# Where operand tiles lie in SBUF: a two-layer attention and FFN trunk on one core

## The chip, the cores and the metric

The kernel runs on one core of a Trainium2 chip. The metric is device time in microseconds. Three runs of the kernel before took 1240.68 to 1240.99 us, median 1240.82.

## What is computed

The input x is 512 tokens by 1024, float32. Two layers follow, each with a mixing half and an FFN half, and a last RMS norm:

```python
for l in range(DEPTH):                                   # 2
    h = rms_norm(x, norm1_g[l])
    rq, rk, rv, rg, sq, sk, sv = split(h @ w_in[l])      # 1024 x 3584
    ret = chunk_retention(rotary(rq), rotary(rk), rv)    # 4 heads of 128
    ret = head_group_norm(ret, ret_norm_g[l]) * silu(rg)
    sb  = head_rms_norm(stick_breaking(sq, sk, sv), sb_norm_g[l])   # 4 heads of 128
    x = x + concat([ret, sb]) @ w_out[l]                 # 1024 x 1024
    h = rms_norm(x, norm2_g[l])
    x = x + (silu(h @ w_gate[l]) * (h @ w_up[l])) @ w_down[l]       # 1024 <-> 2816
return rms_norm(x, final_g)
```

## The kernel before

**Split operands.** Every float32 operand of a large product is kept as two tiles of type fp32r, `hi` and `lo`, made by a ScalarE cast and a VectorE (or GpSimd) subtraction (`split`, L270 to L281). A block of a product is then three matmuls, hi x hi, hi x lo and lo x hi (`mm3`, L181), of 128 x 128 stationary by 128 x 512 moving columns in the projections.

**Stages.** x lies transposed in eight tiles of 128 x 512 (`x0` to `x7`), and so do its gained copies `hhi` and `hlo`. The weights come in 205 units of 1024 columns, in the order of their use (`block_plan`): DMA to `wraw`, split to `whi` and `wlo` three units ahead (`WeightStream`, L94 to L140). In a layer the order is: SV by token; SQ, SK and RG by head; RV by token; RQ and RK by head; the output projection, its first half over the four stick-breaking heads, its second over the four retention heads; then gate and up for 11 of the 22 blocks of the FFN (`f`), down for these, and the same again for the other 11. In the first layer down has the weights stationary and the gated activations (`ahi`, `alo`) moving (L704); in the second the activations are stationary and 512 weight columns moving (`step`, L717).

**Order.** TensorE's program order is written out by hand (`Stream`): the projections are the main stream, and scores, transposes and weighted sums of the heads are side tasks put in after a delay. A scheduler orders the other engines. Each head's scores and weights become pairs (`pthi`, `ptlo`, L438), its result `m` is normed by `shi`, `slo` and a sum over ones (`normed`, L457), and split to `mhi`, `mlo`, which the output projection reads.

**Pools.** A tile pool is a stretch of every partition; pools lie one above the other in the order of their opening. `const`, `keep`, `wpool` and `small` stay; the pools `at0`, `ff0`, `at1` and `ff1` are opened above them one at a time and share the same room. As the built program has it, in KiB from the start of a partition (a 128 x 512 tile takes 2 KiB):

| what | before | after |
|---|---|---|
| scratch that the program reserves for dynamic DMA | 0 to 16 | 0 to 1 |
| constants (`ident`, `ones_r`, ...) | 16 to 19.3 | 1 to 4.3 |
| x | 19.3 to 35.3 | 112.3 to 128.3 |
| `hhi`, `hlo` | 35.3 to 67.3 | 4.3 to 36.3 |
| `ssq`, `rs` | 67.3 to 71.3 | 128.3 to 132.3 |
| `wraw` | 71.3 to 83.3 | 132.3 to 144.3 |
| `whi`, `wlo` | 83.3 to 107.3 | 36.3 to 60.3 |
| temporaries of `small` | 107.3 to 115.7 | 144.3 to 152.7 |
| attention: `vhi`, `vlo` | 127.8 to 143.8 | 60.3 to 76.3 (slots 0 to 7) |
| attention: `qhi`, `qlo`, `khi`, `klo` | 145.8 to 155.8 | 76.3 to 84.3 (slots 8 to 11) |
| attention: `pthi`, `ptlo` | 161.8 to 173.8 | 84.3 to 96.3 (slots 12 to 17) |
| attention: `mhi`, `mlo` of retention heads | 185.8 to 217.8 | 96.3 to 112.3 (slots 18 to 25) |
| attention: `mhi`, `mlo` of stick-breaking heads | 185.8 to 217.8 | 186.8 to 202.8 |
| attention: `shi`, `slo` | 181.8 to 185.8 | 182.8 to 186.8 |
| FFN: `ahi`, `alo`, first layer | 123.8 to 167.8 | 60.3 to 104.3 (slots 0 to 21) |
| FFN: `ahi`, `alo`, second layer | 143.9 to 187.9 | 60.3 to 104.3 (slots 0 to 21) |

Of the kernel before, what the change touches and what calls it, by code (L numbers as in the profile page):

```python
# [10 lines left out]
F32 = mybir.dt.float32  # L11
# [24 lines left out]

# the triangle of score blocks, by bank: block rows of [query, key], and of [key, query]
BY_QUERY = ((3,), (2, 0), (1,))
# [4 lines left out]


def block_plan():
    """Weight blocks in the order of their use: (tensor, layer, k tile, column, width)."""
    plan = []
# [46 lines left out]
class WeightStream:  # L94
    """Loads the weights ahead of their use and splits each into two 12-bit parts."""

    AHEAD = 3

    def __init__(self, nc, pool, ws):
        self.nc, self.pool, self.ws = nc, pool, ws  # L100
        self.units = unit_plan()
        self.raw = []
        self.ready = []
        self.at = (0, 0, 0)

    def load(self, upto, step=UW):
        for i in range(len(self.raw), min(upto, len(self.units))):
            w = sum(b[4] for b in self.units[i])
            raw = self.pool.tile([P, UW], F32, tag="wraw", name=f"wraw{i}", bufs=3)
            for a in range(0, w, step):  # L110
                c = slice(a, min(a + step, w))
                self.nc.sync.dma_start(out=raw[:, c], in_=self.ws[i, :, c])
            self.raw.append((raw, w))
# [28 lines left out]
class Stream:  # L142
    """The order of the tensor engine's work: side tasks are put into the main stream
    when enough of it has passed for their operands to be ready."""

# [53 lines left out]
def layers(ctx, tc, xT_in, ws_in, gcol_in, gfin_in, cos_in, sin_in, dec_in, out):  # L199
    nc = tc.nc  # L200
    const = ctx.enter_context(tc.tile_pool(name="const", bufs=1))
    keep = ctx.enter_context(tc.tile_pool(name="keep", bufs=1))
    wpool = ctx.enter_context(tc.tile_pool(name="wpool", bufs=3))
    small = ctx.enter_context(tc.tile_pool(name="small", bufs=3))
    pp = ctx.enter_context(tc.tile_pool(name="psum", bufs=1, space=PSUM))

    pe = Stream(nc)
    wst = WeightStream(nc, wpool, ws_in)
    NG = 24

    def table(inst):
        """Keeps the scalar engine's table functions in the order of the program."""
        tc.stamp_issue_order_token(inst.ins, "table")
        return inst
# [40 lines left out]

    hhi = [keep.tile([P, S], F32R, name=f"hhi{k}", tag=f"hhi{k}") for k in range(KT)]
    hlo = [keep.tile([P, S], F32R, name=f"hlo{k}", tag=f"hlo{k}") for k in range(KT)]
    ssq = keep.tile([P, S], F32, name="ssq")
# [23 lines left out]
    def feed(k, g):  # L282
        """x tile k is complete: its gained and split copy, and its squares."""
        split(hhi[k], hlo[k], x[k], gcol[:, g + k : g + k + 1])
        if k == 0:
            nc.scalar.activation(out=ssq, in_=x[k], func=AF.Square)
        else:
            q = small.tile([P, S], F32, tag="sqx", name="sqx", bufs=2)
            nc.scalar.activation(out=q, in_=x[k], func=AF.Square)  # L289
            nc.gpsimd.tensor_tensor(out=ssq, in0=ssq, in1=q, op=ALU.add)  # L290

    def rsqrt(out, ss, n, act=nc.scalar.activation):
        """out = (ss / n + eps) ** -0.5, from exp and ln and a Newton step."""
        shape = list(ss.shape)
# [15 lines left out]
    def token_scale():  # L310
        """rs[:, t] = rsqrt(mean of x[t]^2 + eps), the same on every partition."""
        hi, lo = (small.tile([P, S], F32R, tag="sqx", name=n, bufs=2) for n in ("sshi", "sslo"))
        split(hi, lo, ssq)
        ps = bank("o", 1)
        pe.mm(ps, ones_r, hi, True, False)
        pe.mm(ps, ones_r, lo, False, True)
        rsqrt(rs, ps, DM, act)
# [11 lines left out]
    def attention(l):  # L329
        g0 = l * NG  # L330
        with tc.tile_pool(name=f"at{l}", bufs=1, reuse_waits="tile") as sb:
# [25 lines left out]
            def proj_v(col, evac):  # L357
                """[token, column] products, the last k tiles by token block."""
                pss = banks_a() if col == SV else [bank() for _ in range(3)] + [bank("z", 4)]
                v = [  # L360
                    sb.tile([P, TB, S], F32R, tag=n, name=n, bufs=1) for n in ("vhi", "vlo")
                ]
# [11 lines left out]
                for tb in range(TB):  # L374
                    for k, w in ws:
                        step(tb, k, w)
                    done.append(tb)
                    if col == SV and tb == 0:
                        continue
                    if col == SV and tb == 1:  # L380
                        scales()
                    while done:
                        i = done.pop(0)
                        evac(i, pss[i], v[0][:, i], v[1][:, i])
                return v
# [19 lines left out]
            def parts(t, tag):  # L405
                hi = sb.tile([P, S], F32R, tag=tag + "hi", name=tag + "hi", bufs=1)
                lo = sb.tile([P, S], F32R, tag=tag + "lo", name=tag + "lo", bufs=1)
                split(hi, lo, t, eng=nc.gpsimd)
                return t, hi, lo
# [11 lines left out]
            def outer(ps, a, b, ca, cb, last=True):  # L421
                """ps = a[:, ca].T @ b[:, cb] for split a and b."""
                n = cb.stop - cb.start
# [7 lines left out]
            def piece(name, dtype, tag, n, bufs):  # L431
                return sb.tile([P, S], dtype, tag=tag, name=name, bufs=bufs)[:, :n]

            def pair(src):
                n = src.shape[-1]
                hi, lo = (piece(t, F32R, t, n, 3) for t in ("pthi", "ptlo"))
                split(hi, lo, src)
                return hi, lo  # L438

            def weighted(wt, v, h):  # L440
                """o[e, t] = sum over s of v[s, e] wt[s, t], by blocks of s."""
                o = bank("o", 1)
                e = slice(h * HD, h * HD + HD)
                for js, (hi, lo) in zip(BY_KEY, wt):
                    a = 0
                    for j in js:
                        c = slice(a, a + S - j * P)
                        a = c.stop
                        pe.mm3(
                            o[:, j * P :], (v[0][:, j, e], v[1][:, j, e]), (hi[:, c], lo[:, c]),  # L450
                            j == 0, j == BY_KEY[-1][-1],
# [5 lines left out]
            def normed(o, m, key):  # L457
                """m, o by head with its gains, times the rsqrt of o's mean squares."""
                sq = temp("sq")
# [5 lines left out]
                def finish():  # L465
# [5 lines left out]
                    nc.vector.tensor_tensor(out=m, in0=m, in1=rn, op=ALU.mult)  # L471
                    hi = sb.tile([P, S], F32R, tag="mhi", name="mhi", bufs=8)
                    lo = sb.tile([P, S], F32R, tag="mlo", name="mlo", bufs=8)
                    split(hi, lo, m)
# [143 lines left out]
    def ffn(l):  # L618
        last = l == L - 1
        with tc.tile_pool(name=f"ff{l}", bufs=1, reuse_waits="tile") as sb:  # L620
# [39 lines left out]
            def gated(f, pg, pu):  # L660
# [5 lines left out]
                nc.vector.tensor_tensor(out=u, in0=u, in1=g, op=ALU.mult)  # L666
                hi = sb.tile([P, S], F32R, tag=f"ahi{f % FH}", name="ahi")
                lo = sb.tile([P, S], F32R, tag=f"alo{f % FH}", name="alo")
                split(hi, lo, u)
# [127 lines left out]
```

## Time and profile before

| | |
|---|---|
| median of 3 runs | 1240.82 us |
| span of the profiled execution, first to last instruction | 1238.8 us |
| TensorE (PE) busy | 1220.4 us, 99% |
| PE weight loads (PEld), beside the matmuls | 999.2 us, 81% |
| VectorE (DVE), ScalarE (ACT), GpSimd (POOL) busy | 56%, 39%, 13% |
| mean granted clock of TensorE | 0.994 |

The profile shows one execution, whose own time is its span; the median of the runs is 2.0 us above it. Matmuls are pipelined, so the "mean ns" of a matmul (some 390 ns) counts a good part of its time together with the next one's. The pace of a row of matmuls is read from start to start: the time between the starts of the first and of a later one, by the number of matmuls between them.

### The profile page before, as it was taken

To read this page: it belongs to the slowest core of one execution; us is meant where nothing else is said; L and a number is where in the kernel's file an instruction comes from. 1 tells how busy PE (TensorE), PEld (TensorE's weight loads), DVE (VectorE), ACT (ScalarE), POOL (GpSimd) and SP (SyncE) were. 2 spreads that over 40 slices of the span, in tenths; PEclk is the share of its full clock that TensorE was granted. 3 is DMA by queue.
4 is the path that set the end of the run, shared out by engine and by line. 5 is a ranking of instruction groups with operands and counts; after the bars stand their busy time and mean duration, and the time that the engine had idled before them with its cause. 6 is when DMAs were issued, how large, how long until landed. Compare 5 with 4: busy or idle time off the path is not lost.

```text
span 1238.8 us, 13898 instructions
## 1 busy us (share of the span) xinstructions
PE 1220.4 (99%) x5474; PEld 999.2 (81%) x5474; DVE 693.5 (56%) x861; ACT 488.8 (39%) x708; POOL 165.7 (13%) x142
## 2 busy tenths in 40 slices
PE   8999999999999999999999999999999999999997
PEld 5888887888888888888888888878888888888886
DVE  5557799775443244444444778997644433444433
ACT  5557553453322123223334766345432312223323
POOL 3221154130000000000112212422100000000011
PEclk9999999999999999999999999999999999999999
DMA  6221231232322323322232222223322322332221
GB/s 238 86 80 57 85 102 58 80 101 87 102 100 87 102 86 101 102 93 96 91 129 86 69 69 85 85 69 102 103 85 89 99 83 94 113 102 87 101 85 69
DMA packets 33329, 115.74 MB, mean 93 GB/s; under 512 B 3824, under 2 KB 3824, under 8 KB 33264
## 3 DMA queue, kind: packets, MB, share of 16 engines
q1 hardware_dynamic: 33120, 114.83, 28.1%
q8 instruction: 43, 0.70, 0.2%
q14 instruction: 22, 0.18, 0.0%
q10 hardware_dynamic: 144, 0.02, 0.0%
HBM read 112.75 MB, written 2.10 MB: 93 GB/s over the span
## 4 chain that ended last, share of the span: by engine, by line
PE 94%; DVE 4%; issue 1%; DMA 1%; ACT 1%; POOL 0%; SPq 0%; DVEq 0%; ACTq 0%
PE acc L178 72%; PE z L178 16%; PE o L178 5%; PE z L189 1%; DMA wraw<-ws 1%; DVE ptlo L274 1%; DVE wlo L125 1%; DVE hlo L277 0%; DVE u L300 0%; DVE mlo L274 0%; POOL slo L274 0%; DVE m L561 0%; DVE t L416 0%; DVE t L414 0%; DVE p L552 0%
## 5 line engine op out<-in xcount | busy, mean ns | idle before, releaser
L124 ACT CAST whi<-wraw 128x1024 fp32r<-128x1024 f32 (+1 forms) x205 | 214.6, 1047 | 505.7 <-PE acc L178 237.2
L178 PE MATMUL acc<-hhi,whi 128*128 128x512 f32 x960 | 376.0, 392 | 0.0
L178 PE MATMUL acc<-hhi,wlo 128*128 128x512 f32 x960 | 373.9, 389 | 0.0
L178 PE MATMUL acc<-hlo,whi 128*128 128x512 f32 x960 | 373.6, 389 | 0.0
L125 DVE TENSOR_TENSOR wlo<-wraw,whi 128x1024 fp32r<-128x1024 f32 (+1 forms) x205 | 258.1, 1259 | 135.8 <-ACT whi L124 134.7
L178 PEld LDWEIGHTS acc<-hhi,wlo 128*128 128x128 f32 x960 | 180.2, 188 | 37.8
L178 PEld LDWEIGHTS acc<-hhi,whi 128*128 128x128 f32 x960 | 180.3, 188 | 36.2
L178 PEld LDWEIGHTS acc<-hlo,whi 128*128 128x128 f32 x960 | 180.3, 188 | 36.0
L665 DVE TENSOR_TENSOR u<-acc,rs 128x512 f32<-128x512 f32 x40 | 27.7, 692 | 134.5 <-PE acc L178 134.5
L290 POOL TENSOR_TENSOR ssq<-ssq,sqx 128x512 f32<-128x512 f32 x28 | 44.8, 1600 | 397.0 <-ACT sqx L289 396.3
L662 DVE TENSOR_TENSOR g<-acc,rs 128x512 f32<-128x512 f32 x40 | 27.7, 692 | 89.9 <-PE acc L178 89.9
L178 PE MATMUL acc<-ahi,wlo 128*128 128x512 f32 x176 | 69.8, 396 | 0.0
L178 PE MATMUL acc<-alo,whi 128*128 128x512 f32 x176 | 69.8, 396 | 0.0
L178 PE MATMUL acc<-ahi,whi 128*128 128x512 f32 x176 | 69.8, 396 | 0.0
L730 POOL TENSOR_TENSOR xtd<-xtd,gfin 128x512 f32<-128x512 f32 x7 | 10.1, 1447 | 349.3 <-ACT fsq L726 349.3
L277 DVE SCALAR_TENSOR_TENSOR hlo<-x,gcol,hhi 128x512 fp32r<-128x512 f32 x32 | 38.6, 1224 | 9.0 <-ACT hhi L276 9.0
L178 PEld LDWEIGHTS acc<-alo,whi 128*128 128x128 f32 x176 | 33.1, 188 | 8.1
L178 PEld LDWEIGHTS acc<-ahi,whi 128*128 128x128 f32 x176 | 33.1, 188 | 8.1
L178 PEld LDWEIGHTS acc<-ahi,wlo 128*128 128x128 f32 x176 | 33.1, 188 | 8.1
L273 ACT CAST ahi<-u 128x512 fp32r<-128x512 f32 x44 | 27.3, 621 | 28.1 <-DVE u L666 28.1
L178 PE MATMUL acc<-mhi,wlo 128*128 128x512 f32 x88 | 36.2, 411 | 0.0
L178 PE MATMUL acc<-mlo,whi 128*128 128x512 f32 x88 | 36.0, 409 | 0.0
(189 smaller groups left out, 1819.0 us busy)
## 6 DMA issues: line engine op xcount, KB each, us to landing
wraw<-ws SPq DMA_DIRECT2D x203, 512.0 KB, 3.5
x<-xT SPq DMA_DIRECT2D x8, 256.0 KB, 7.4
dec<-dec SPq DMA_DIRECT2D x8, 256.0 KB, 4.1
out<-ob SPq DMA_DIRECT2D x4, 512.0 KB, 2.6
wraw<-ws SPq DMA_DIRECT2D x2, 256.0 KB, 3.8
cosrs<-cos SPq DMA_DIRECT2D x2, 256.0 KB, 5.3
sinrs<-sin SPq DMA_DIRECT2D x2, 256.0 KB, 5.4
gfin<-gfin SPq DMA_DIRECT2D x1, 512.0 KB, 4.5
```

Of the source, the lines that this page charges most:

```text
L124: nc.scalar.copy(out=hi[:, c], in_=raw[:, c])
L125: nc.vector.tensor_tensor(out=lo[:, c], in0=raw[:, c], in1=hi[:, c].bitcast(F32), op=ALU.subtract)
L178: self.nc.tensor.matmul(ps, lhsT=lhsT, rhs=rhs, start=start, stop=stop)
L189: self.nc.tensor.transpose(out, src, ident)
L273: nc.scalar.copy(out=hi, in_=src)
L274: eng.tensor_tensor(out=lo, in0=src, in1=hi.bitcast(F32), op=ALU.subtract)
L277: eng.scalar_tensor_tensor(out=lo, in0=src, scalar=scale, in1=hi.bitcast(F32), op0=ALU.mult, op1=ALU.subtract,)
L290: nc.gpsimd.tensor_tensor(out=ssq, in0=ssq, in1=q, op=ALU.add)
L662: nc.vector.tensor_tensor(out=g, in0=pg, in1=rs, op=ALU.mult)
L665: nc.vector.tensor_tensor(out=u, in0=pu, in1=rs, op=ALU.mult)
L730: nc.gpsimd.tensor_tensor(out=y, in0=y, in1=gfin[:, c], op=ALU.mult)
```

## The change

Three new pools stand below `keep`: `hpool` takes `hhi` and `hlo`, `wpool` keeps only `whi` and `wlo`, and `low` has 26 slots of 128 x 512. The slots take the tiles `vhi`, `vlo` (now four tiles each, one for each block of 128 tokens), `qhi` to `klo`, `pthi`, `ptlo` and the retention heads' `mhi`, `mlo` in attention, and the activations `ahi`, `alo` in the FFN. x, `ssq`, `rs`, `wraw` and all temporaries come above them. The scratch for dynamic DMA goes from 16 KiB to 1 KiB. Not moved down are the stick-breaking heads' `mhi`, `mlo`, the tiles `shi`, `slo`, and the float32 tiles that TensorE transposes or reads whole (`e`, `q`, `k`, x, `ssq`). No operation is added or removed. The diff, cut:

```diff
     const = ctx.enter_context(tc.tile_pool(name="const", bufs=1))
+    hpool = ctx.enter_context(tc.tile_pool(name="hpool", bufs=1))
+    wpool = ctx.enter_context(tc.tile_pool(name="wpool", bufs=3))
+    low = ctx.enter_context(tc.tile_pool(name="low", bufs=1))
     keep = ctx.enter_context(tc.tile_pool(name="keep", bufs=1))
-    wpool = ctx.enter_context(tc.tile_pool(name="wpool", bufs=3))
+    rawpool = ctx.enter_context(tc.tile_pool(name="rawpool", bufs=3))
...
+V_SLOT, QK_SLOT, PT_SLOT, M_SLOT = 0, 8, 12, 18
+    def slot(i, name):
+        return low.tile([P, S], F32R, tag=f"slot{i}", name=name)
...
-            raw = self.pool.tile([P, UW], F32, tag="wraw", name=f"wraw{i}", bufs=3)
+            raw = self.rawpool.tile([P, UW], F32, tag="wraw", name=f"wraw{i}", bufs=3)
...
-    hhi = [keep.tile([P, S], F32R, name=f"hhi{k}", tag=f"hhi{k}") for k in range(KT)]
+    hhi = [hpool.tile([P, S], F32R, name=f"hhi{k}", tag=f"hhi{k}") for k in range(KT)]
...
                 v = [
-                    sb.tile([P, TB, S], F32R, tag=n, name=n, bufs=1) for n in ("vhi", "vlo")
+                    [slot(V_SLOT + TB * i + tb, n) for tb in range(TB)]
+                    for i, n in enumerate(("vhi", "vlo"))
                 ]
...
-                hi, lo = (piece(t, F32R, t, n, 3) for t in ("pthi", "ptlo"))
+                at = PT_SLOT + 2 * (pairs[0] % 3)
+                pairs[0] += 1
+                hi, lo = slot(at, "pthi")[:, :n], slot(at + 1, "ptlo")[:, :n]
...
-                    hi = sb.tile([P, S], F32R, tag="mhi", name="mhi", bufs=8)
-                    lo = sb.tile([P, S], F32R, tag="mlo", name="mlo", bufs=8)
+                    if key < NH:
+                        hi, lo = (slot(M_SLOT + 2 * key + i, n) for i, n in enumerate(("mhi", "mlo")))
+                    else:
+                        hi = sb.tile([P, S], F32R, tag="mhi", name="mhi", bufs=4)
+                        lo = sb.tile([P, S], F32R, tag="mlo", name="mlo", bufs=4)
...
-                hi = sb.tile([P, S], F32R, tag=f"ahi{f % FH}", name="ahi")
-                lo = sb.tile([P, S], F32R, tag=f"alo{f % FH}", name="alo")
+                hi, lo = slot(2 * (f % FH), "ahi"), slot(2 * (f % FH) + 1, "alo")
...
-    nc = bacc.Bacc("TRN2", target_bir_lowering=False, num_devices=1)
+    nc = bacc.Bacc("TRN2", target_bir_lowering=False, num_devices=1, dynamic_dma_scratch_size=1024)
```

TensorE's instructions and GpSimd's stand in the same order as before. On the other engines the scheduler moves a few. On VectorE, at the start of the first layer's RQ and RK projections, the rows before are these (`wlo21` to `wlo23` are splits of weight units, `rn` belongs to the norm of the last stick-breaking head, `t1` and `t2` to the rotation of the first RQ head):

```order
L274 TENSOR_TENSOR vlo_1137<-vtmp_1324,vhi_1136 128x512
L399 TENSOR_TENSOR vtmp_1344<-vtmp_1344,mu_1346 128x512
L300 SCALAR_TENSOR_TENSOR u_1376<-r_1375 128x512
L303 SCALAR_TENSOR_TENSOR u_1376<-o_1371,u_1376 128x512
L274 TENSOR_TENSOR vlo_1137<-vtmp_1344,vhi_1136 128x512
L306 SCALAR_TENSOR_TENSOR rn_1374<-u_1376,r_1375 128x512
L414 TENSOR_TENSOR t1_1399<-acc_1352,cosrs_203 128x512
L125 TENSOR_TENSOR wlo23_1412<-wraw23_1357,whi23_1411 128x1024
L415 TENSOR_TENSOR t2_1400<-acc_1352,sinrs_204 64x512
```

and in the changed kernel, at the same place of the same engine, they are these:

```order
L285 TENSOR_TENSOR vlo_1157<-vtmp_1345,vhi_1153 128x512
L411 TENSOR_TENSOR vtmp_1365<-vtmp_1365,mu_1367 128x512
L311 SCALAR_TENSOR_TENSOR u_1397<-r_1396 128x512
L285 TENSOR_TENSOR vlo_1158<-vtmp_1365,vhi_1154 128x512
L314 SCALAR_TENSOR_TENSOR u_1397<-o_1392,u_1397 128x512
L128 TENSOR_TENSOR wlo23_1433<-wraw23_1378,whi23_1432 128x1024
L317 SCALAR_TENSOR_TENSOR rn_1395<-u_1397,r_1396 128x512
L426 TENSOR_TENSOR t1_1420<-acc_1373,cosrs_212 128x512
L427 TENSOR_TENSOR t2_1421<-acc_1373,sinrs_213 64x512
```

The split `wlo23` moved ahead of `rn` and `t1`, and stands ahead of `t2` in both; a few rows earlier `wlo21` moved behind one subtraction, and on ScalarE two small casts moved ahead of the cast of a weight unit. The second layer has the same moves. On the DMA queue of SyncE, towards the end of the first layer's FFN, the loads of the next layer's rotation tables (`cosrs`, `sinrs`) and of the first two decay tables (`dec`) stood here before:

```order
L112 DMA wraw105_4653<-ws 128x1024
L112 DMA wraw106_4683<-ws 128x1024
L340 DMA cosrs_4640<-cos 128x512
L341 DMA sinrs_4641<-sin 128x512
L537 DMA dec_5963<-dec 128x512
L537 DMA dec_6096<-dec 128x512
L112 DMA wraw107_4713<-ws 128x1024
```

and stand here now:

```order
L115 DMA wraw95_4307<-ws 128x1024
L115 DMA wraw96_4342<-ws 128x1024
L351 DMA cosrs_4661<-cos 128x512
L352 DMA sinrs_4662<-sin 128x512
L556 DMA dec_5996<-dec 128x512
L556 DMA dec_6129<-dec 128x512
L115 DMA wraw97_4379<-ws 128x1024
```

They moved ahead of ten weight loads; the load of `gfin` in the second layer moved ahead of two.

## Rows read from the trace of the kernel before

**Rows 1.** The page, part 1: busy us (share of the span) and instructions

```profile
span 1238.8 us, 13898 instructions
PE 1220.4 (99%) x5474; PEld 999.2 (81%) x5474; DVE 693.5 (56%) x861; ACT 488.8 (39%) x708; POOL 165.7 (13%) x142
```

**Rows 2.** The page, part 4: the chain that ended last, by engine

```profile
PE 94%; DVE 4%; issue 1%; DMA 1%; ACT 1%; POOL 0%; SPq 0%; DVEq 0%; ACTq 0%
```

**Rows 3.** Waits of TensorE: who waited for whom, us in total, times, longest

```profile
PE z L178 <- DVE wlo L125: 3.2, 3, 2.7
PE o L178 <- ACT shi L273: 2.6, 2, 1.3
PE o L178 <- POOL slo L274: 2.1, 2, 1.1
```

**Rows 4.** Timeline of TensorE (start us, busy us): where FFN stretches begin

```profile
377.01 0.40 PE L178 MATMUL acc<-ahi,whi 128*128 128x512 f32 x1
...
438.85 0.39 PE L178 MATMUL acc<-hhi,whi 128*128 128x512 f32 x1
...
558.55 0.40 PE L178 MATMUL acc<-ahi,whi 128*128 128x512 f32 x1
...
620.39 0.39 PE L178 MATMUL z<-whi,hhi 128*128 128x512 f32 x1
...
988.29 0.39 PE L178 MATMUL acc<-whi,ahi 128*128 128x512 f32 x1
...
1049.88 0.39 PE L178 MATMUL acc<-hhi,whi 128*128 128x512 f32 x1
...
1169.58 0.39 PE L178 MATMUL acc<-whi,ahi 128*128 128x512 f32 x1
...
1230.94 0.40 PE L178 MATMUL z<-whi,alo 128*128 128x512 f32 x1
```

**Rows 5.** Groups by line, 438.85 to 558.5 and 377.01 to 438.8 us: one of three

```profile
L178 PE MATMUL acc<-hhi,whi 128*128 128x512 f32 x176 | 68.5, 389 | 0.0
...
L178 PE MATMUL acc<-ahi,whi 128*128 128x512 f32 x88 | 34.9, 396 | 0.0
```

**Rows 6.** Stretches: length, busy us of PE, PEld, DVE, ACT, POOL; PEclk, DMA, GB/s

```profile
378.00:438.00 60.00, 60.00 (x258) 48.24 (x257) 19.32 (x20) 11.22 (x12) 0.00 (x0) 1.00 0.29 95
440.00:558.00 118.00, 118.00 (x522) 97.76 (x521) 53.41 (x63) 34.17 (x42) 0.00 (x0) 1.00 0.30 98
```

**Rows 7.** Timeline of TensorE: output projection of the first layer, and a side task

```profile
227.85 0.39 PE L178 MATMUL o<-pthi,vhi 128*128 128x512 f32 x1
...
228.54 0.33 PE L178 MATMUL o<-pthi,vhi 128*128 128x384 f32 x1
...
236.51 0.39 PE L178 MATMUL z<-mhi,whi 128*128 128x512 f32 x1
...
256.80 0.39 PE L178 MATMUL z<-hhi,whi 128*128 128x512 f32 x1
```

**Rows 8.** Groups of ScalarE by line: high addresses only, low addresses only

```profile
L273 ACT CAST ahi<-u 128x512 fp32r<-128x512 f32 x44 | 27.3, 621 | 28.1 <-DVE u L666 28.1
L289 ACT ACTIVATE sqx<-x 128x512 f32<-128x512 f32 x28 | 17.1, 616 | 0.0
```

**Rows 9.** The page, part 5: splits of the weights, and projections that read the hi tiles

```profile
L124 ACT CAST whi<-wraw 128x1024 fp32r<-128x1024 f32 (+1 forms) x205 | 214.6, 1047 | 505.7 <-PE acc L178 237.2
L178 PE MATMUL acc<-hhi,whi 128*128 128x512 f32 x960 | 376.0, 392 | 0.0
...
L125 DVE TENSOR_TENSOR wlo<-wraw,whi 128x1024 fp32r<-128x1024 f32 (+1 forms) x205 | 258.1, 1259 | 135.8 <-ACT whi L124 134.7
```

**Rows 10.** Waits of SyncE's DMA queue: us in total, times, longest

```profile
SPq L112 <- DVE wlo L125: 1088.4, 197, 12.3
```

**Rows 11.** A stretch of the first layer: length, PE busy; PEclk, DMA share, GB/s

```profile
204.00:207.00 3.00, 3.00 (x9) 0.55 0.00 0
```

More of the change, by code (lines that the diff above doesn't have):

```diff
@@ L97, with __init__ @@
     AHEAD = 3
-    def __init__(self, nc, pool, ws):
-        self.nc, self.pool, self.ws = nc, pool, ws
+    def __init__(self, nc, pool, rawpool, ws):
+        self.nc, self.pool, self.rawpool, self.ws = nc, pool, rawpool, ws
         self.units = unit_plan()
@@ L207, in layers @@
     pe = Stream(nc)
-    wst = WeightStream(nc, wpool, ws_in)
+    wst = WeightStream(nc, wpool, rawpool, ws_in)
+    def slot(i, name):
+        return low.tile([P, S], F32R, tag=f"slot{i}", name=name)
     NG = 24
@@ L254, in layers @@
     )
-    hhi = [keep.tile([P, S], F32R, name=f"hhi{k}", tag=f"hhi{k}") for k in range(KT)]
-    hlo = [keep.tile([P, S], F32R, name=f"hlo{k}", tag=f"hlo{k}") for k in range(KT)]
+    hhi = [hpool.tile([P, S], F32R, name=f"hhi{k}", tag=f"hhi{k}") for k in range(KT)]
+    hlo = [hpool.tile([P, S], F32R, name=f"hlo{k}", tag=f"hlo{k}") for k in range(KT)]
     ssq = keep.tile([P, S], F32, name="ssq")
@@ L383, in proj_v @@
                         i = done.pop(0)
-                        evac(i, pss[i], v[0][:, i], v[1][:, i])
+                        evac(i, pss[i], v[0][i], v[1][i])
                 return v
@@ L405, in parts @@
             def parts(t, tag):
-                hi = sb.tile([P, S], F32R, tag=tag + "hi", name=tag + "hi", bufs=1)
-                lo = sb.tile([P, S], F32R, tag=tag + "lo", name=tag + "lo", bufs=1)
+                at = QK_SLOT + 2 * "qk".index(tag)
+                hi, lo = slot(at, tag + "hi"), slot(at + 1, tag + "lo")
                 split(hi, lo, t, eng=nc.gpsimd)
@@ L432, in piece @@
                 return sb.tile([P, S], dtype, tag=tag, name=name, bufs=bufs)[:, :n]
+            pairs = [0]
             def pair(src):
                 n = src.shape[-1]
-                hi, lo = (piece(t, F32R, t, n, 3) for t in ("pthi", "ptlo"))
+                at = PT_SLOT + 2 * (pairs[0] % 3)
+                pairs[0] += 1
+                hi, lo = slot(at, "pthi")[:, :n], slot(at + 1, "ptlo")[:, :n]
                 split(hi, lo, src)
@@ L449, in weighted @@
                         pe.mm3(
-                            o[:, j * P :], (v[0][:, j, e], v[1][:, j, e]), (hi[:, c], lo[:, c]),
+                            o[:, j * P :], (v[0][j][:, e], v[1][j][:, e]), (hi[:, c], lo[:, c]),
                             j == 0, j == BY_KEY[-1][-1],
```

## The prediction

> **What bounds the kernel now.** I read the busy times first, then the chain, then TensorE's waits. TensorE is busy 1220.4 of 1238.8 us [rows 1], and the chain that ended last is 94% TensorE [rows 2]. Its three largest waits sum to 3.2 + 2.6 + 2.1 = 7.9 us in the whole span [rows 3]. So the end is set by how fast TensorE takes one matmul after the other, and a change that alters no instruction of it can only act through that pace or through waits.
>
> The pace is not in the mean durations, which overlap; it is read from start to start. Gate and up of the first layer's second half run from 438.85 to 558.55 us [rows 4] with 3 x 176 = 528 matmuls [rows 5]: 119.70 / 528 = 226.7 ns. Down of the half before runs from 377.01 to 438.85 us [rows 4] with 3 x 88 = 264 matmuls of the same shape [rows 5]: 61.84 / 264 = 234.2 ns. In the second layer down takes 1049.88 - 988.29 = 61.59 us for 264 [rows 4], 233.3 ns.
>
> What differs? Both stretches have TensorE at full clock and without a gap, and the same DMA share, 0.29 and 0.30; the faster one has the busier neighbours, VectorE at 53.41 / 118 = 45% against 19.32 / 60 = 32%, ScalarE at 29% against 19% [rows 6]. So the slower pace isn't other engines' traffic. The pattern is the same too, three matmuls per block. What is left is where the operands lie. Gate and up read `hhi`, `hlo` and the split weights, all between 35 and 107 KiB of the partition; down reads `ahi`, `alo` between 124 and 188 KiB, moving in the first layer and stationary in the second (the names in [rows 4] stand as moving, stationary). The second half of the output projection, whose moving `mhi`, `mlo` lie above 185 KiB, bears it out: from 236.51 to 256.80 us [rows 7] stand 87 matmuls of 512 columns (the 96 of the half less 9 already past), 20.29 / 87 = 233.2 ns. No row tells whether the upper part itself is slow or the distance between the two operands; the change brings both down, so it doesn't matter here. Nor does a row tell where the step lies, only that it is between 107.3 KiB (end of `wlo`) and 123.8 (first `ahi`). The slots end at 112.3; were the step right at 107.3, the last retention head's `mhi` and `mlo` would stay slow, 2 x 24 matmuls, 0.3 us.
>
> **The change, part by part.** I take 226.7 ns for a matmul both of whose operands come to lie in the lower part.
>
> Down, four stretches: at that pace 264 matmuls take 59.85 us. The first layer's two took 61.84 each (377.01 to 438.85, 558.55 to 620.39), the second's 61.59 and, for 263 intervals, 1230.94 - 1169.58 = 61.36 against 59.62 [rows 4]. Gain 1.99 + 1.99 + 1.74 + 1.74 = 7.46 us. TensorE has no gap there and nothing else waits, so it comes whole.
>
> Output projection: only the retention heads' half moves down, 96 matmuls a layer: 2 x 96 x (233.2 - 226.7) ns = 1.25 us. The stick-breaking half, as many, keeps its pace.
>
> Scores and weighted sums, 32 tasks: the three matmuls of 512 columns in one go at (228.54 - 227.85) / 3 = 230 ns [rows 7], 3.3 ns over the fast pace: 32 x 3 x 3.3 ns = 0.3 us. The narrower ones could gain too: a task of about 1.9 us by the same 2.8% that the output projection gains, 32 tasks, 1.7 us; the low end is nothing. I take 0.3, the value of its own row.
>
> What moves up: x, raw weights, temporaries. ScalarE's pass over 128 x 512 takes 621 ns with both sides high and 616 ns with both sides low [rows 8], so its work and VectorE's keep their times. If the 205 weight casts took 5 ns more each, that were 1 us of ScalarE, covered by its idle time of 505.7 us ahead of just these casts, most of it waiting for TensorE to free a buffer [rows 9]. x's 32 transposes, slowed as down is, would cost 32 x 7.5 ns = 0.2 us. I put both at nothing.
>
> The moved instructions: on VectorE a split of 1259 ns [rows 9] goes ahead of `rn` and `t1`. Behind `rn` waits the last stick-breaking head's `mhi`, read in the output projection; GpSimd's sum of `t1` and `t2` is no later, since `t2` stood behind that split before. The weight unit behind a small cast comes some 0.6 us later [rows 8]; TensorE's only wait for splits is 3.2 us in three times [rows 3], and three units are ahead. On the DMA queue four small loads pass ten weight loads; the queue waits 1088.4 us for VectorE to free raw buffers [rows 10], so it has time, and no wait in front of these four is new. `v` in four tiles makes waits finer, not later. Price of all this: nothing; if the cover were gone, one late split, 1.3 us a layer.
>
> The waits for `shi` and `slo` stay, since the chain through ScalarE and GpSimd isn't touched. After them the granted clock averages 0.55 from 204 to 207 us [rows 11], 9 matmuls in 3.00 us where 13 fit at 226.7: 4 x 0.227 = 0.9 us there. If TensorE reaches them sooner, it waits longer by that much, at most the 0.3 us of the tasks; a lost or gained wait with its slow clock is worth up to (2.6 + 2.1) / 2 + 0.9 = 3.3 us a layer.
>
> Sum: 7.46 + 1.25 + 0.3 = 9.0 us. The profiled span becomes 1238.8 - 9.0 = 1229.8; the median stands 2.0 us above the span, so 1240.8 - 9.0 = 1231.8 us.
>
> **Rivals.** *The place has no part in it.* Then the time stays at 1240.8. For it: no row shows one and the same matmul with its operand low and high, and the slow ones also share that their operand was made a short while before. Against it: in down each activation tile is read eight times, over 61.8 us, and the pace doesn't recover; and `hhi` is made anew four times without being slow. [...]
>
> *The bottom of the partition is slow as well.* `hhi` and `hlo` go from 35 to 67 KiB down to 4 to 36, from where no 512-column fp32r operand was streamed before. If they took on down's pace there, 3 x 960 = 2,880 matmuls [rows 9] would lose 6.9 ns each, 19.9 us: 1231.8 + 19.9 = 1251.7, slower. It decides from 9.0 / 0.0069 = 1,300 such matmuls on. Against it: `hhi0` to `hlo7` and the weights stream evenly over 72 KiB.
>
> *Only the moving operand counts, or waits eat a part.* Then the second layer's 3.48 us, where the activations are stationary, don't come: 1235.3. Against it: that stretch is slow now with its moving operand low.
>
> **How the numbers follow.** Forecast as summed 0.80; no effect 0.09; slow bottom 0.05; part of it 0.06. A measurement of this kernel tells a change from none at about 0.2%, 2.5 us. The forecast and the part are faster by more: 0.86. No effect gives 0.08 within 0.2% and, with its last hundredth and the slow bottom, 0.06 slower. The likeliest one's own range is 1229.0 (tasks gain 1.7 instead of 0.3, and 1.4 of the 3.3 that a wait with its clock is worth goes) to 1234.4 (a late split in each layer adds 2.6). Taking in the partial case, 1235.3 with one late split of 2.6, the range is 1229.0 to 1238.0; left out are no effect and the slow bottom, 0.14.
>
> **What would show it.** Right: starts 226 to 228 ns apart in all four down stretches (some 59.9 us for 264) and in the second half of the output projection; gate and up unchanged at 119.7 us; the stick-breaking half of the output projection still near 233; the waits for `shi` and `slo` as now. Wrong: down at 234 with its activations low (no effect); gate and up longer than 119.7 us (slow bottom); only the first layer's down shorter (moving operand alone); a new wait of TensorE for `whi` or `wlo` behind the start (the moved splits).

## The result, and the profile after

The changed kernel takes 1232.32 us (median of 4 runs, 1231.52 to 1232.77) against 1240.75 us of the kernel before (4 runs, 1239.48 to 1240.99), a ratio of 0.9935 with an interval of 0.9921 to 0.9949. Its profiled execution has a span of 1229.7 us, where 1229.8 was forecast; the median was forecast at 1231.8. So the size came out as predicted. The cause given for it did not, as the experiments show.

Part 1 of the page after (busy us, share of the span, instructions) stands against [rows 1]:

```profile
span 1229.7 us, 13902 instructions
...
PE 1211.7 (99%) x5474; PEld 999.1 (81%) x5474; DVE 693.4 (56%) x861; ACT 489.4 (40%) x708; POOL 164.9 (13%) x142
```

TensorE has 5474 matmuls as before and is busy 8.7 us less; the work is the same and its pace is another. Where the pace changed, the timeline tells, row by row as in [rows 4]:

```profile
376.14 0.39 PE L181 MATMUL acc<-ahi,whi 128*128 128x512 f32 x1
...
435.98 0.39 PE L181 MATMUL acc<-hhi,whi 128*128 128x512 f32 x1
...
555.66 0.39 PE L181 MATMUL acc<-ahi,whi 128*128 128x512 f32 x1
...
615.50 0.39 PE L181 MATMUL z<-whi,hhi 128*128 128x512 f32 x1
...
982.66 0.39 PE L181 MATMUL acc<-whi,ahi 128*128 128x512 f32 x1
...
1042.50 0.39 PE L181 MATMUL acc<-hhi,whi 128*128 128x512 f32 x1
...
1162.18 0.39 PE L181 MATMUL acc<-whi,ahi 128*128 128x512 f32 x1
...
1221.79 0.39 PE L181 MATMUL z<-whi,alo 128*128 128x512 f32 x1
```

The first down stretch now lasts 435.98 - 376.14 = 59.84 us for 264 matmuls, 226.7 ns each, and so do the second and third; the last takes 59.61 for 263 intervals. Gate and up between the first two takes 555.66 - 435.98 = 119.68 us, as before. With the same reading of the other starts the whole span falls apart so:

| stretch | before, us | after, us | difference |
|---|---|---|---|
| up to the first projection | 6.18 | 6.50 | +0.32 |
| attention, both layers | 388.94 | 389.00 | +0.06 |
| output projection, first layer | 52.86 | 51.83 | -1.03 |
| output projection, second layer | 52.86 | 52.00 | -0.86 |
| gate and up, four stretches | 483.47 | 483.33 | -0.14 |
| down, four stretches | 246.63 | 239.13 | -7.50 |
| behind the last row of the timeline | 7.86 | 7.91 | +0.05 |
| span | 1238.8 | 1229.7 | -9.1 |

The neighbours are as busy as before. These are the stretches of [rows 6] after (length; busy time and count of PE, PEld, DVE, ACT, POOL; granted clock, DMA share, GB/s):

```profile
377.00:435.00 58.00, 58.00 (x257) 48.02 (x257) 19.26 (x21) 11.38 (x12) 0.00 (x0) 1.00 0.29 97
437.00:555.00 118.00, 118.00 (x523) 97.69 (x522) 53.51 (x63) 34.19 (x43) 0.00 (x0) 1.00 0.29 98
```

In down 257 matmuls now stand in 58 us, before 258 in 60; in gate and up nothing moved.

TensorE's waits after, against [rows 3] (who waited for whom; us in total, times, longest):

```profile
PE o L181 <- ACT shi L284: 2.6, 2, 1.3
PE z L181 <- DVE wlo L128: 2.4, 1, 2.4
PE o L181 <- POOL slo L285: 2.1, 2, 1.1
...
PE z L181 <- POOL klo L285: 0.5, 1, 0.5
```

The waits for `shi` and `slo` are the same to a tenth. The one for `wlo` fell from 3.2 to 2.4 us, one for `whi` rose from 0.5 to 0.9, and one for `klo` is new.

### The profile page after: what moved, and what is told of

Read it like the earlier page. It is cut to its first block, busy times and chain, and to the rows that moved or that the text cites. A ratio compares the mean times of both kernels' runs of the same rounds, so it can differ in the third digit from the quotient of the medians.

```text
span 1229.7 us, 13902 instructions
## 1 busy us (share of the span) xinstructions
PE 1211.7 (99%) x5474; PEld 999.1 (81%) x5474; DVE 693.4 (56%) x861; ACT 489.4 (40%) x708; POOL 164.9 (13%) x142
## 4 chain that ended last, share of the span: by engine, by line
PE 93%; DVE 4%; issue 2%; POOL 1%; DMA 1%; ACT 1%; SPq 0%; DVEq 0%; ACTq 0%; POOLq 0%
PE acc L181 71%; PE z L181 16%; PE o L181 4%; PE z L192 1%; DMA wraw<-ws 1%; DVE ptlo L285 1%; DVE wlo L128 1%; DVE hlo L288 0%; DVE u L311 0%; DVE mlo L285 0%; POOL slo L285 0%; DVE m L580 0%; DVE t L428 0%; DVE t L426 0%; DVE p L571 0%
## 5 line engine op out<-in xcount | busy, mean ns | idle before, releaser
L181 PE MATMUL z<-wlo,hhi 128*128 128x512 f32 x80 | 32.8, 410 | 2.4 <-DVE wlo L128 2.4
L181 PE MATMUL acc<-mhi,whi 128*128 128x512 f32 x88 | 35.1, 399 | 0.0
```

Of the source, the lines that this page charges most:

```text
L181: self.nc.tensor.matmul(ps, lhsT=lhsT, rhs=rhs, start=start, stop=stop)
```

## The experiments

In each, the four down stretches are read as above; 59.84 us (59.61 for the last) is the fast pace, 61.1 to 61.9 the slow one. Edits named "from before" change the kernel before, the others the changed kernel.

**e1_slots_across.** The change's own theory was a step in the partition. Here the slots are put above `keep` and the raw weights, at 92.3 to 144.3 KiB, so that the upper of them lie where the activations were slow.

```
     wpool = ...
-    low = ctx.enter_context(tc.tile_pool(name="low", bufs=1))
     keep = ...
     rawpool = ...
+    low = ctx.enter_context(tc.tile_pool(name="low", bufs=1))
```

> The changed kernel with its slots moved up by 32 KiB (x, ssq, rs and raw weights below them), so that they run from 92.3 to 144.3 KiB and the FFN activations of f = 0 to 4 lie below 112.3 KiB, those of f = 5 to 10 above. Theory (an operand above a step somewhere between 112.3 and 123.8 KiB is slow): in each down group of 33 matmuls the first 15 come 227 ns apart and the later ones 231 to 238, from the first f above the step on; with the step at 112 KiB 18 of 33 are slow, a stretch of 264 takes 59.84 + 144 x 7.0 ns = 60.8 us, the output projection's retention half is slow again (1.25 us), and the time is 1232.3 + 4.0 + 1.25 = 1237.6 us. With the step at 120 KiB only f = 7 to 10 are slow, 1236. Rival (place has no part, the 16 KiB of scratch or the room above does it): all stretches stay at 59.8 us, 1232.3.

Measured: 1231.22 us (one run), and down in its first stretch (timeline of TensorE)

```profile
375.87 0.39 PE L181 MATMUL acc<-ahi,whi 128*128 128x512 f32 x1
...
435.71 0.39 PE L181 MATMUL acc<-hhi,whi 128*128 128x512 f32 x1
```

59.84 us, as are the second and third. Activations up to 136.3 KiB are fast, so the step that was sought between 107.3 and 123.8 KiB doesn't exist, and the 1237.6 us expected by it did not come.

**e2_both_high.** Two readings were left of "where the operands lie": the upper part is slow, or the distance between the two operands is. Here `hhi`, `hlo` (112.8 to 144.8 KiB) and the split weights (144.8 to 168.8) lie high and the slots below them (44.8 to 96.8). The edit, in short:

```
-    hpool, wpool, low    (below keep)
     keep, rawpool, small
+    low
+    padpool.tile([P, 4096], F32, name="pad")
+    hpool, wpool
     psum
```

> The changed kernel with its pools in another order: x, raw weights, small temporaries and the slots below 96.8 KiB, then hhi and hlo at 112.8 to 144.8 and the split weights at 144.8 to 168.8 KiB. Projections that read hhi and hlo then have both operands high, down and the retention half one high and one low. Theory A (a high operand is slow as such): gate and up 528 matmuls in some 123.3 us instead of 119.7, every projection 6.8 ns slower, 4,704 of them that are fast now: 1232.3 + 32 = 1264 us. Theory B (only two operands on different sides are slow): gate and up stay at 119.7 us, down goes to 61.6 to 61.8 and the retention half to 233 ns, the stick-breaking half becomes fast: 1232.3 + 7.5 + 1.25 - 1.25 = 1239.8 us. If place has no part: 1232.3.

Measured: 1231.17 us, ratio 0.9933 (0.9918 to 0.9948). Its timeline:

```profile
375.67 0.39 PE L181 MATMUL acc<-ahi,whi 128*128 128x512 f32 x1
...
435.51 0.39 PE L181 MATMUL acc<-hhi,whi 128*128 128x512 f32 x1
...
555.19 0.39 PE L181 MATMUL acc<-ahi,whi 128*128 128x512 f32 x1
```

Down takes 59.84 us and gate and up 119.68 with all their operands but the slots above 112 KiB, where 1264 or 1239.8 us were expected by the two readings. Neither height nor distance shows in these times.

**e3_scratch_alone** (from before): only the smaller scratch, which shifts every tile down by 15 KiB.

```
-    nc = bacc.Bacc("TRN2", target_bir_lowering=False, num_devices=1)
+    nc = bacc.Bacc("TRN2", target_bir_lowering=False, num_devices=1, dynamic_dma_scratch_size=1024)
```

> The kernel before with the scratch of 1 KiB alone: every tile lies 15 KiB lower, the first layer's activations of f = 0 at 108.8 to 112.8 KiB, the others above. Theory (step at about 112 KiB): 3 of 33 matmuls a group become fast in the first layer, 2 x 24 x 7 ns = 0.3 us, so 1240.4 us. Rival (the scratch's size or where it lies matters by itself): a good part of the 8.4 us comes, 1232 to 1237.

Measured: 1239.56 us in one run (1240.29 for the kernel before beside it), down 61.84, 61.84, 61.59, 61.36 us as in [rows 4]. The scratch has no part in the gain.

**e4_first_layer_high.** The first layer's activations go back to a pool of the FFN, at 160.8 to 204.8 KiB; the second layer's stay in the slots.

```
-                hi, lo = slot(2 * (f % FH), "ahi"), slot(2 * (f % FH) + 1, "alo")
+                if last:
+                    hi, lo = slot(2 * (f % FH), "ahi"), slot(2 * (f % FH) + 1, "alo")
+                else:
+                    hi = sb.tile([P, S], F32R, tag=f"ahi{f % FH}", name="ahi")
+                    lo = sb.tile([P, S], F32R, tag=f"alo{f % FH}", name="alo")
```

> The changed kernel with the activations of the first layer alone taken back to the FFN's own pool at 160.8 to 204.8 KiB; all else is low. Theory (place): the first layer's two down stretches take 61.8 us again, the second layer's stay at 59.84: 1232.3 + 4.0 = 1236.3 us. Rival (place has no part): 1232.3.

Measured: 1236.25 us, ratio 0.9969 (0.9956 to 0.9981). The timeline of its first and third down:

```profile
376.89 0.40 PE L181 MATMUL acc<-ahi,whi 128*128 128x512 f32 x1
...
438.74 0.39 PE L181 MATMUL acc<-hhi,whi 128*128 128x512 f32 x1
...
987.48 0.39 PE L181 MATMUL acc<-whi,ahi 128*128 128x512 f32 x1
...
1047.32 0.39 PE L181 MATMUL acc<-hhi,whi 128*128 128x512 f32 x1
```

61.85 us in the first layer and 59.84 in the second: just what the theory of place expects. Yet place had fallen in e2. What else did going back alter? In the built programs the start addresses differ in their last digits. Here the first layer's activations start at 0 modulo 256 bytes and the weights at 96; in e1 both start at 96, in e2 both at 0. The new theory: a matmul is fast when its two operands start alike, modulo 128 or 256 bytes. In the same programs small tiles, those of `small`, `rst` and `fss`, of 4 to 16 bytes, take 32 bytes each and so set where what lies above them begins. In the kernel before, `hhi`, `hlo` and the weights start at 96, the activations at 0 in the first layer and at 128 in the second; in the changed kernel `wpool` and the slots follow `hhi` in steps of 2 KiB, and all start at 96.

**f1_before_padded** (from before): only pads, no pool moved.

```
+    const.tile([P, 8], F32, name="pad_c")
...
+    const.tile([P, 24], F32, name="pad_k")
...
+            sb.tile([P, 16], F32, name="pad_a")      # attention, behind rst
...
+            sb.tile([P, 24], F32, name="pad_f")      # FFN, first in its pool
```

> The kernel before, every tile in its old order and high up as it was, with four pads of 32 to 96 bytes in its pools, so that the start address of every float32 and fp32r operand of TensorE is 96 bytes over a multiple of 128 (before: hhi, hlo and the split weights 96, ahi and alo 0, the attention tiles 32, ones_r 64). Theory (the pace is slow where the moving and the stationary operand start at different places within 128 bytes): all four down stretches 59.84 us (7.5 us in all), both halves of the output projection fast (2.5 us), tasks 0.3: 1240.3 - 10.3 = 1230.0 us, better than the changed kernel, whose stick-breaking half stays at 233 ns. Rival (place in the partition): nothing changes, 1240.3.

Measured: 1234.62 us, ratio 0.9951 (0.9938 to 0.9963), in part a miss. Its timeline:

```profile
376.85 0.39 PE L178 MATMUL acc<-ahi,whi 128*128 128x512 f32 x1
...
436.69 0.39 PE L178 MATMUL acc<-hhi,whi 128*128 128x512 f32 x1
...
982.76 0.40 PE L178 MATMUL acc<-whi,ahi 128*128 128x512 f32 x1
...
1044.12 0.40 PE L178 MATMUL acc<-hhi,whi 128*128 128x512 f32 x1
```

The first layer is fast, 59.84 us, with activations and weights both at 224; the second keeps 61.36. I had aligned modulo 128 only: there the four `fss` tiles leave the activations at 96 and the weights at 224, 128 bytes apart. So either 256 is the period, or the theory is wrong; the next runs tell.

**f5_low_off_32.** The changed kernel with its slots 32 bytes higher, still low and next to the weights.

```
     low = ctx.enter_context(tc.tile_pool(name="low", bufs=1))
+    low.tile([P, 8], F32, name="pad_l")
```

> The changed kernel with a pad of 32 bytes ahead of its slots: all of them stay in the lower 112 KiB, 32 bytes higher, at 0 within 128 bytes while hhi, hlo and the split weights stay at 96. Theory (different places within 128 bytes): down at 61.84 and 61.6 us again, the retention half at 233 ns, 1232.3 + 7.5 + 1.25 + 0.1 = 1241 us: all that the change brought is lost with 32 bytes. Rival (place in the partition): 1232.3.

Measured: 1239.90 us, ratio 0.9993 (0.9984 to 1.0002). All of the gain is gone. Its first down:

```profile
377.09 0.40 PE L181 MATMUL acc<-ahi,whi 128*128 128x512 f32 x1
...
438.69 0.40 PE L181 MATMUL acc<-hhi,whi 128*128 128x512 f32 x1
```

61.60 us. Nothing of the place has changed; 32 bytes have.

**f2_off_128_256.** Wider slots, in which the activations start 128 bytes in for the first half of a layer's blocks and 256 for the second.

```
-        return low.tile([P, S], F32R, tag=f"slot{i}", name=name)
+        return low.tile([P, S + 128], F32R, tag=f"slot{i}", name=name)[:, off // 4 : off // 4 + S]
...
+                off = ((128, 256), (128, 256))[l][f // FH]
```

> The changed kernel with slots of 2,560 bytes, in which the FFN activations start 128 bytes (first half of a layer's blocks) or 256 bytes (second half) into the slot. Theory (places within 128 bytes): nothing changes, all four down stretches 59.84 us, 1231 to 1232.5 us. If the length that counts is 256 bytes, the first down of each layer is slow (61.8 and 61.6), the second not; if it is 512, all four are slow, 1240.

Measured: 1235.59 us (one run). The first layer's two halves on its timeline:

```profile
377.31 0.40 PE L181 MATMUL acc<-ahi,whi 128*128 128x512 f32 x1
...
438.90 0.39 PE L181 MATMUL acc<-hhi,whi 128*128 128x512 f32 x1
...
558.60 0.39 PE L181 MATMUL acc<-ahi,whi 128*128 128x512 f32 x1
...
618.44 0.39 PE L181 MATMUL z<-whi,hhi 128*128 128x512 f32 x1
```

61.59 us at 128 bytes, 59.84 at 256; the second layer has 61.36 and 59.61. So 256 bytes bring the pace back and 128 do not; the expectation by 128 bytes missed, the one by 256 held.

**f3_off_16_96_64.** The same slots with 16 and 96 bytes in the first layer (activations moving), 64 and 16 in the second (stationary).

```
+                off = ((16, 96), (64, 16))[l][f // FH]
```

> The same with the activations 16 and 96 bytes in (first layer's two down stretches, moving operand) and 64 and 16 bytes in (second layer's, stationary operand). Theory (places within 128 bytes, to a grain of 16 bytes or less): all four slow, 61.8, 61.8, 61.6 and 61.4 us, 1232 + 7.5 = 1239.5 us. If the grain is 32 bytes, the two with 16 bytes are at 59.84 and the time is 1235.7. If only 0 against 32 were slow, for the moving operand alone, fewer.

Measured: 1236.24 us (one run). The halves with 16 bytes, first layer and then second:

```profile
375.73 0.40 PE L181 MATMUL acc<-ahi,whi 128*128 128x512 f32 x1
...
436.88 0.39 PE L181 MATMUL acc<-hhi,whi 128*128 128x512 f32 x1
...
1166.89 0.39 PE L181 MATMUL acc<-whi,ahi 128*128 128x512 f32 x1
...
1226.50 0.39 PE L181 MATMUL z<-whi,alo 128*128 128x512 f32 x1
```

61.15 us with the moving operand 16 bytes off, a little below the slow pace; 59.61 with the stationary one 16 bytes off, the fast pace. At 96 and 64 bytes it is slow (61.62, 61.60). So neither all four are slow nor both with 16 bytes fast, as the two expectations had it; why 16 bytes differ by operand stays open.

**g1_before_aligned** (from before): f1 with two pads more suited, so that all operands of matmuls of 512 columns start at 96 modulo 256 bytes, while the activations stay above 120 KiB.

```
+    const.tile([P, 8], F32, name="pad_c")
...
+    const.tile([P, 56], F32, name="pad_k")
...
+            sb.tile([P, 16], F32, name="pad_a")
...
+            sb.tile([P, 24], F32, name="pad_f")
...
+                sb.tile([P, 32], F32, name="pad_s")  # last layer, behind fss
```

> The kernel before with five pads (32 to 224 bytes), every tile in its old order and place but for these bytes: all fp32r and float32 operands of TensorE now start 96 bytes over a multiple of 256. Theory (the pace is slow where moving and stationary operand start at different places within 256 bytes): four down stretches at 59.84 us (59.6 for the last), both halves of the output projection at 227 ns: 1240.4 - 7.5 - 2.5 - 0.3 = 1230.1 us. Rival (the place in the partition has a part of its own): the activations at 124 to 188 KiB keep some of their loss, 1232 to 1240.

Measured: 1230.69 us (5 runs), ratio 0.9926 (0.9914 to 0.9939). The second layer's first down, which f1 had missed:

```profile
981.83 0.39 PE L178 MATMUL acc<-whi,ahi 128*128 128x512 f32 x1
...
1041.67 0.39 PE L178 MATMUL acc<-hhi,whi 128*128 128x512 f32 x1
```

59.84 us, like the others. Five pads, and not one pool moved, give all that the change gave.

**g2_after_aligned.** The changed kernel with `pad_c`, `pad_k` and `pad_a` of g1, which bring the stick-breaking heads' `mhi`, `mlo` from 32 to 96 too.

```
+    const.tile([P, 8], F32, name="pad_c")
...
+    const.tile([P, 56], F32, name="pad_k")
...
+            sb.tile([P, 16], F32, name="pad_a")
```

> The changed kernel with three pads, by which the operands that it left high (stick-breaking mhi and mlo, shi, slo, x, e, q, k) also start 96 bytes over a multiple of 256. Theory (256 bytes): the stick-breaking half of the output projection goes from 233 to 227 ns, 1.25 us, and the norm's sums 0.1: 1232.3 - 1.35 = 1231.0 us at the most, and the same as the kernel before with its pads within a microsecond, low or high. Rival (place): the stick-breaking half stays at 233 ns, 1232.3.

Measured: 1231.12 us, ratio 0.9927 (0.9914 to 0.9939). In the stick-breaking half of the output projection 32 matmuls without a gap, on the timeline of the changed kernel

```profile
219.76 0.39 PE L181 MATMUL acc<-mhi,whi 128*128 128x512 f32 x1
...
227.22 0.39 PE L181 MATMUL acc<-mhi,wlo 128*128 128x512 f32 x1
```

and on that of this one

```profile
220.10 0.39 PE L181 MATMUL acc<-mhi,whi 128*128 128x512 f32 x1
...
227.38 0.39 PE L181 MATMUL acc<-mhi,wlo 128*128 128x512 f32 x1
```

take 7.46 and 7.28 us, 233.1 and 227.5 ns each. The output projections shorten to 51.48 and 51.46 us, 0.9 us in all, in which the slow clock and a wait of the one execution or the other have a part (see the output projection below). Of 1231 us that is less than the times can tell from nothing: the interval overlaps that of the changed kernel.

**g3_projections_off** (from before): the theory turned round. 32 bytes between `hlo` and what follows put the weights at 128 and leave `hhi`, `hlo` at 96, so that the stretches that were fast should turn slow.

```
     hlo = [keep.tile([P, S], F32R, name=f"hlo{k}", tag=f"hlo{k}") for k in range(KT)]
+    keep.tile([P, 8], F32, name="pad_h")
```

> The kernel before with one pad of 32 bytes between hlo and ssq: hhi and hlo stay at 96 within 256 bytes, the split weights go to 128, and no operand pair of the projections, of down or of the output projection starts alike. Theory (256 bytes): gate and up, 528 matmuls, go from 119.7 to some 123.3 us, and all 3,456 matmuls that read hhi or hlo lose 6.8 ns: 1240.4 + 23.5 = 1264 us. Rival (place): 32 bytes change nothing, 1240.4.

Measured: 1258.68 us (one run), 18.4 us over the kernel before beside it (1240.24). Gate and up of the first layer's second half:

```profile
443.49 0.40 PE L178 MATMUL acc<-hhi,whi 128*128 128x512 f32 x1
...
566.69 0.39 PE L178 MATMUL acc<-ahi,whi 128*128 128x512 f32 x1
```

123.20 us for 528, 233.3 ns, where it was 119.70. The four such stretches lose 13.7 us, near the 14.4 expected. Attention loses only 1.2 us in the first layer and 3.2 in the second of some 4.5 each that were expected. In the first layer the clock gave some of it back: from 24 to 27 us the kernel before has 8 matmuls at a granted clock of 0.53, this one 14 at 1.00, some 1.4 us. Why the rest falls short is not settled.

**g4_after_again.** The changed kernel as it is, beside g1 and g2.

> The changed kernel as it is, timed beside the two kernels with pads on the same chip: 1232.3 us by every theory, 1.3 to 2.2 us above them by the theory of 256 bytes, level with them by the rival.

Measured: 1232.11 us (5 runs, 1229.64 to 1232.74), ratio 0.9936 (0.9923 to 0.9950). The result repeats. It lies 1.4 and 1.0 us above g1 and g2, the way that the theory of 256 bytes has it, but the intervals overlap.

All down stretches together, by how far the activations start past the weights modulo 256 bytes. The times are read from the timelines of the runs named, from start to start, and the starts of the tiles from their built programs:

| bytes | operand that the activations are | kernels | us for 264 matmuls | ns each |
|---|---|---|---|---|
| 0 | moving and stationary | changed, e1, e2, e4, f1, f2, g1, g2, g4 | 59.84 | 226.7 |
| 16 | moving / stationary | f3 | 61.15 / 59.61 for 263 | 231.6 / 226.7 |
| 32 | stationary / moving | before, e3, f5, g3 / f5 | 61.59 / 61.60 | 233.3 |
| 64 | stationary | f3 | 61.60 | 233.3 |
| 96 | moving | f3 | 61.62 | 233.4 |
| 128 | moving / stationary | f2 / f1, f2 | 61.59 / 61.36 | 233.3 / 232.4 |
| 160 | moving | before, e3, e4, g3 | 61.84 | 234.2 |

Pairs that are equal at 0 (e2), at 96 and at 224 (f1) are equally fast, 59.84 us: in these runs the time goes with the relation of the two starts, not with a place of either.

Whose starts, is not fully told. In each of these stretches all moving operands start alike and all stationary ones do. So a matmul's own pair can't be told there from the pair of its moving operand and the next matmul's stationary one, whose load runs beside it: in the changed kernel the first matmul of down starts at 376.14 us, the next one's weight load at 376.15. The two pairs part where a task breaks into the projections. At 20 such places a matmul whose operands both start at 96 is followed by one of 512 columns whose operands start elsewhere, but alike. With the follower at 32 (before) the starts lie 227.5 ns apart on the mean, with the follower at 128 (f5) 233.4. So in these two runs what comes next counts too, and a follower at another start was not always slow: "both operands of a matmul alike" describes whole stretches, and is not shown for single matmuls.

## Why the prediction was right, and where it was wrong

**The number.** 9.0 us were forecast; 9.1 came in the span and 8.4 between the medians. Of the terms, down is 7.50 for 7.46. That the sums agree to 0.1 us is in part luck: the output projection gave 0.64 more than forecast, by the clock of this execution, the tasks nothing for 0.3, and the first projection began 0.32 later.

**The output projection.** 1.25 were forecast and 1.89 came. The retention half runs at (255.96 - 236.11) / 87 = 228.2 ns, not at 226.7, mainly as one of its matmuls, at 242.47 us, waits for the split of its `mlo` (its weight load stands idle for 0.26 us), so that 331 ns pass before the next start. That makes 2 x 96 x 5.0 ns = 0.96 us. The rows of the first layer, for [rows 7]:

```profile
236.11 0.39 PE L181 MATMUL z<-mhi,whi 128*128 128x512 f32 x1
...
255.96 0.39 PE L181 MATMUL z<-hhi,whi 128*128 128x512 f32 x1
```

The rest stands in front of that half. The stretch behind the wait, [rows 11], reads after (length; PE busy and count; granted clock, DMA share, GB/s)

```profile
204.00:207.00 3.00, 3.00 (x14) 1.00 0.00 0
```

14 matmuls at the full clock for 9 at 0.55, so the first layer's slow clock is absent here. It lasted longer than the 3 us from which the prediction took 0.9 us: the first twelve matmuls of the stick-breaking half took 4.34 us before (from 203.94) and take 2.80 now (from 204.13), 1.54 less. Half of that is given back, since TensorE now comes too early for `klo`:

```profile
214.68 0.40 PE L181 MATMUL z<-qlo,khi 128*128 128x512 f32 x1
215.55 0.50 PE L181 MATMUL z<-qhi,klo 128*128 128x512 f32 x1 [0.47 <-POOL klo L285]
```

These two take 0.75 us more from start to start than before, and the two matmuls that read `shi` and `slo` behind them 0.18 more. In the second layer the slow clock is there (0.50 from 806.9 to 809.0 us), but the same twelve take 3.93 us for 4.34, and nothing waits for `klo`. In the same kernel's second profile (g4_after_again) it is the other way round: the clock is 0.54 from 203 to 206 us and 1.00 from 806.9 to 809.0, and the wait for `klo` stands in the second layer. So the slow clock and this wait belong to the execution and not to the change.

**The tasks.** 0.3 us were forecast, of which attention shows nothing: +0.06 us. In the built programs `pthi`, `ptlo` and `vhi`, `vlo` start alike before (all at 32) and after (all at 96), so by the new theory there was nothing to gain. A trio still takes (228.15 - 227.46) / 3 = 230 ns, as in [rows 7]:

```profile
227.46 0.39 PE L181 MATMUL o<-pthi,vhi 128*128 128x512 f32 x1
...
228.15 0.34 PE L181 MATMUL o<-pthi,vhi 128*128 128x384 f32 x1
```

**What was costed at nothing** cost nothing that can be seen: the new wait for `klo` goes with the clock, as just said, the waits for splits of weights changed by less than a microsecond, and gate and up kept their pace. The prediction called 3.2 us TensorE's only wait for splits and overlooked one of 0.5 us for `whi`. It also took `sqx` for a tile on the low side, though it lay at 107.3 to 111.3 KiB, in the gap in which the step was sought; nothing hung on it, as ScalarE is busy 488.8 us before and 489.4 after.

**The step that failed** is "What is left is where the operands lie", with what hung on it: the step that was to lie between 107.3 and 123.8 KiB, and "the change brings both down, so it doesn't matter here". It did matter. The rows told that one and the same shape has two paces without a wait, 226.7 and 234.2 ns, and that neighbours and clock do not set them; from there I took the first property in which the operands differed, their height, and listed no other. Their start modulo 256 bytes was another, to be had from the built program like the table of places. e1 and e2 show that place has no part (59.84 us in the first down of both), f5 that 32 bytes undo the change (61.60 us), g1 that pads give it without a move (59.84 us). By luck the new order of pools aligned just those tiles that it brought down, and left the stick-breaking heads' `mhi`, `mlo` at 32, so that the wrong cause and the right one gave the same sum; the change with one tile of 32 bytes in front of the slots would have been forecast at 1231.8 and measured at 1239.9.

**The rivals.** "The place has no part in it" was true in its words and wrong in its time, 1240.8: the changed kernel took 1232.32 us, and the runs show two paces, 226.7 ns where the operands start alike and 233.3 where they are 32 bytes apart (f5). "Only the moving operand counts" is refuted by the second layer, which gained 3.50 us with its activations stationary. "The bottom is slow" did not occur: gate and up with `hhi` from 4.3 KiB on took 119.68 us.

Open are what in the chip makes the pace depend on the starts, whether it is a matmul's own two operands or its neighbours' that decide, the grain below 32 bytes, and whether matmuls narrower than 512 columns or of other types show it.

## What to carry to other kernels

Read the pace of TensorE from start to start and compare stretches of one shape; two paces without a wait between (here 226.7 and 232.4 to 234.2 ns) are a question of their own. Before explaining them by place, list every property of the operands' addresses, the start modulo 256 bytes among them: in this kernel's built program tiles of 4 to 16 bytes shift what lies above them by 32 bytes each, and five pads were enough to put it right (g1, 1230.69 us for 1240.24). When a change moves tiles and the time falls, shift them by 32 bytes before believing in the move (f5 went back to 1239.90 us).

## What the runs showed of the hardware that was not expected

- In the down stretches of this kernel's runs (the table above) matmuls of 128 x 512 in fp32r, each with its own stationary operand, start every 226.7 ns where both operands start alike modulo 256 bytes and every 232.4 to 234.2 ns where they are 32 to 160 bytes apart, 2.5 to 3.3% more. The granted clock was 1.00 at 234.2 ns (before, [rows 6]) and at 226.7 (the changed kernel, 377 to 435 us). At 16 bytes it was 231.6 ns with the moving operand shifted and 226.7 with the stationary one (f3).
- The fast pace was measured from 4.3 KiB of the partition (`hhi` in the changed kernel: gate and up 119.68 us for 528) to above 160 KiB (`ahi`, `alo` of the second layer in g1, up to 188.3 KiB: down 59.84 us for 264), and with the activations moving as with them stationary (first and third down of the changed kernel, 59.84 us each).
- Where TensorE's clock stayed at 1.00 behind the waits for `shi` and `slo`, the 1.54 us that this saved came back by half, 0.75 us from start to start, as a longer wait for `klo` (changed kernel, first layer, 1.00 from 204 to 207 us where it was 0.55 before).
- 32 bytes between two tiles of the kernel before cost 18.4 us (g3), and pads of at most 224 bytes gained 9.6 us (g1: 1240.24 to 1230.69). The first is a single run.
